# Top-k selection steps tied on VectorE behind mixer B's value evictions and key/query scalings

## The chip, the core and the metric

The kernel runs on one core of a Trainium2 chip. The metric is the device time of one execution in microseconds (us). Each kernel is run several times and the median is compared. Within a core, TensorE (PE) multiplies matrices into PSUM, VectorE (DVE) and ScalarE (ACT) work element by element, GpSimd (POOL) does the same more slowly and issues some transfers, and SyncE (SP) issues the others. Each engine works through its own list of instructions in order; semaphores tie the lists together.

## The reference

Two layers are computed on a sequence of 512 tokens of width 1024, in float32. A layer projects the normalised input with one wide matrix, feeds two attention mixers, merges them through sigmoid gates, and ends in a gated feed-forward part with a short convolution. What matters here is how the two mixers depend on the projection:

```python
# mixer A: sparse attention over the top 128 keys of each query
score = jnp.einsum('bths,bth->bts', rel, wi) * idx_scale
score = jnp.where(admissible[None], score, -jnp.inf)
_, sel = lax.top_k(score, topk)
...
# mixer B: latent attention, dense over the causal chunks
kv = (ckv @ b_w_ukv[l]).reshape(B, S, B_HEADS, B_NOPE + B_V)
kb = jnp.concatenate([kv[..., :B_NOPE], k_rope], axis=-1)
vb = kv[..., B_NOPE:]
qb = rms_norm(qb, b_q_norm[l])
kb = rms_norm(kb, b_k_norm[l])
y_b = latent_attention(qb, kb, vb)
```

The selection (`top_k`) needs only the indexer's scores, which are ready early in the layer, and its result is used only when mixer A starts. Mixer B lies between the two.

## The kernel before, in words

Every float32 product is split in a high and a low part, so that one product becomes three matmuls. PE therefore has a dense stream of matmuls with up to 512 columns. The low part of each operand is a subtraction on DVE (`split_into`, L312 to L318, `Weights.split`, L194), so that DVE stands behind nearly every operand that PE uses.

The program is written as several generators that are advanced in turn: a *filler* (`mix_dense`) that emits the projections piece by piece, the mixers (`scores_b`, `values`, `turn_b`), and the selection (`top_k`). A Tile scheduler then orders each engine's list by this emission order and by its own idea of when operands are ready. What an engine does next is thus set before the kernel runs, and the chip follows the lists.

In each layer this order holds around the change:

- The indexer's scores go into the tiles `sc`, for three query blocks with 512, 384 and 256 admissible keys. Block 0 needs no selection.
- `top_k` finds the 128 largest scores of each row, eight at a time, in 16 rounds. A round has six steps on DVE: three `V.max` (L1036, tile `m`), which find the eight largest, and three `V.match_replace` (L1043, tile `sc`), which mark them as taken. At the end three steps (L1047) turn the marks into the additive mask `sel`. These are 99 steps per layer.
- `side_0` hands out selection steps while the filler runs towards mark `b0`. It hands out `RATE_0` = 1 step for each piece of the filler. In this stretch lie four gate tiles `gb`, and then `attn_b(0)`, which makes mixer B's keys, values and queries for heads 0 to 3. Its four value tiles go through PSUM tag `L`, which has three banks. ACT copies the keys and the high part of the values, DVE takes the low part of the values (`vb`, L315), and the bank is free when both are done. The same banks hold the query tiles (L893) and later the attention scores.
- After that mixer B runs. `Feeder` advances the filler (the rest of `attn_b`, the gates, mixer A's first projections) and hands out `RATE_T` = 0.2 selection steps per call. Whatever is left is handed out before mixer A starts.
- `sel` is read first by POOL, in `bias_a` (L1115), for mixer A's first head.

Keys and queries are scaled on DVE (L880, tile `kn`, and L924, tile `qn`) and then transposed by PE (L1149), split (`tbh`, `tbl`), and multiplied into scores (L1164 to L1166). The rows' largest scores come from DVE (L1167, `mx`), the exponentials from ACT (L369, `P`), the division from DVE (L1063), and PE transposes the result (L1074).

Of the kernel before, what the change touches and what calls it, by code (L numbers as in the profile page):

```python
# [10 lines left out]
F32 = mybir.dt.float32  # L11
# [4 lines left out]
OP = mybir.AluOpType  # L16
# [23 lines left out]

RATE_B = [0.85, 0.55, 0.75, 0.55]
RATE_A = [0.95, 1.05, 0.65, 0.95]
RATE_T = 0.2
LAG_S = 22
LAG_T = 4
GAP_B = 12
# [17 lines left out]
VL = 0  # L64
TAIL = 1
TAIL_3 = 3
PK = 0
RATE_0 = 1
DL = ['gb', 'ga', 'uv', 'ug', 'kv', 'uq']
DN1 = []  # L70
DN2 = []
# [175 lines left out]
def trunk(ctx: ExitStack, tc: tile.TileContext, xT, wd, vecs, bias, rot_n, outT):  # L247
# [61 lines left out]
        split_into(h, o, src, scale, lag)  # L309
        return h, o  # L310

    def split_into(h, o, src, scale=None, lag=1):  # L312
        if scale is None:
            A.copy(h, src)
            later(lag, lambda: V.tensor_tensor(out=o, in0=src, in1=h.bitcast(F32), op=OP.subtract))  # L315
        else:
            A.activation(h, src, AF.Copy, scale=scale)
            later(lag, lambda: V.scalar_tensor_tensor(o, src, scale, h.bitcast(F32), op0=OP.mult, op1=OP.subtract))  # L318
# [253 lines left out]
    def mix_dense(l, nrm):  # L572
# [260 lines left out]
        def attn_b(g):  # L833
# [12 lines left out]
            while len(st.get("ckvl", ())) < 2:  # L846
                yield
            h, o = W.get("kv", g)
            for t in range(4):
                ts = slice(t * 128, (t + 1) * 128)  # L850
                p = bank(BB)
                xs = [(st["ckvh"][k][:, ts], st["ckvl"][k][:, ts]) for k in range(2)]
                seq = ([(x, h, k) for k in range(2) for x in xs[k]] + [(xs[k][0], o, k) for k in range(2)] if "k" in LO
                       else [q for k in range(2) for q in ((xs[k][0], h, k), (xs[k][1], h, k), (xs[k][0], o, k))])
                for n, (x, w, k) in enumerate(seq):
                    mm(p, lhsT=x, rhs=w[:, k * 512:(k + 1) * 512], start=n == 0, stop=n == 5, skip_group_check=True)
                    if n == 2:
                        yield
                if t == 3:
                    W.ahead()  # L860
                p = p.rearrange("p (h c) -> p h c", c=64)
                A.copy(k4[t][:, :, 0:64], p[:, 0:4])
                v = vb[t].rearrange("p (h c) -> p h c", c=128)
                split_into(v[:, :, 0:64], v[:, :, 64:128], p[:, 4:8])
                squares(p[:, 0:4], ssk[:, t], 64)
                yield

            def keys():
# [5 lines left out]
                def scale():  # L874
                    for t in range(4):
# [1 line left out]
                                        in0=st["kr"][:, t:t + 1, :].to_broadcast([128, 4, 32]),  # L877
                                        in1=r[:, t, :, None].to_broadcast([128, 4, 32]), op=OP.mult)
                        G.tensor_copy(k4[t][:, :, 96:100], late_k[:, t:t + 1, :].to_broadcast([128, 4, 4]))
                        (G if "K" in POOL else V).tensor_tensor(out=k4[t][:, :, 0:64], in0=k4[t][:, :, 0:64],  # L880
                                        in1=r[:, t, :, None].to_broadcast([128, 4, 64]), op=OP.mult)
                later(LAG_S, scale)
            later(3, keys)
# [32 lines left out]
            def queries():  # L916
# [4 lines left out]

                def scale():
                    for t in range(4):
                        (G if "Q" in POOL else V).tensor_tensor(out=q4[t][:, :, 0:96], in0=q4[t][:, :, 0:96],  # L924
                                        in1=r[:, t, :, None].to_broadcast([128, 4, 96]), op=OP.mult)
                later(LAG_S, scale)
            later(3, queries)
            st["b", g] = (qn, kn, vb)
# [100 lines left out]
    def top_k():  # L1029
# [3 lines left out]
        for _ in range(TOPK // 8):  # L1033
            for i in (3, 2, 1):
                with low():
                    ins = V.max(out=m8[i], in_=st["sc"][i][:, :128 * (i + 1)])  # L1036
                if PK and i == 3 and "v" in tables:
                    tc.add_manual_dep(ins.ins, tables["v"].ins.name, no_sync, reason="spread")
                yield
            for i in (3, 2, 1):  # L1040
                s = st["sc"][i][:, :128 * (i + 1)]
# [190 lines left out]
    for l in range(DEPTH):  # L1232
# [10 lines left out]

        fl.fill(GAP_I)
        weave([index_scores()], lambda: fl.fill(1))
        tk = top_k()

        def side_tk(n):
# [6 lines left out]
        due = [0.0]  # L1255

        def side_0():
            due[0] += RATE_0
            side_tk(int(due[0]))
            due[0] %= 1  # L1260

# [389 lines left out]
```

## Time and profile before

| what | value |
|---|---|
| time, median of 3 runs | 1537.66 us (1537.4 to 1538.77) |
| profiled execution | 1536.24 us, span 1534.5 us |
| PE busy | 1525.7 us (99% of the span) |
| PEld (weight load) busy | 1335.7 us (87%) |
| DVE busy | 1124.4 us (73%) |
| ACT busy, POOL busy | 946.3 us (62%), 396.3 us (26%) |
| granted TensorE clock | 1.00 |

Layer 0 lies at about 0 to 780 us of the span, layer 1 behind it. In layer 0 the selection runs from about 53 us to 177 us, mixer B's first value tile is multiplied at about 91 us, and mixer A's first head begins at about 224 us. In layer 1 the same stretch lies between about 810 us and 985 us.

A row of the timeline gives start and duration in us, then engine, line, operation, output and inputs, shape and count. Matmuls overlap, so that the distance from start to start, not the duration, is what one costs. In square brackets stands the idle time of the engine ahead of the row, and what ended it. A row of the windows gives, for a stretch, the busy time of PE, PEld, DVE, ACT and POOL, each with its count of instructions, then the granted clock, the DMA share and GB/s.

### The profile page before, as it was taken

What the parts mean: (1) busy time and instruction counts of PE and PEld (TensorE: products, weight loads), DVE (VectorE), ACT (ScalarE), POOL (GpSimd) and SP (SyncE); (2) the same over time, 40 slices, a digit from 0 to 9 for tenths busy, and PEclk for the clock granted to TensorE, in tenths of its full rate; (3) what the DMA queues carried; (4) which work ended last, traced back from release to release, by engine and by line L of the source; (5) the groups of instructions that cost most, each with busy time, mean ns of one, the idle gap of its engine ahead of it and who ended that gap; (6) DMA issues with size and microseconds to landing.
All of it is one profiled execution on the core that took longest, in us unless ns stands there. A gap on an engine that the chain in (4) does not pass through costs nothing.

```text
span 1534.5 us, 23946 instructions
## 1 busy us (share of the span) xinstructions
PE 1525.7 (99%) x8658; PEld 1335.7 (87%) x8658; DVE 1124.4 (73%) x2305; ACT 946.3 (62%) x1553; POOL 396.3 (26%) x578
## 2 busy tenths in 40 slices
PE   9999999999999999999999999999999999999999
PEld 8887999888888898889998889998888888988899
DVE  7899988666476693547979999886674857835586
ACT  7756668773577536664557576687635765456642
POOL 2343012400011442124602520223001115311364
PEclk9999999999999999999999999999999999999999
DMA  7464124733488438873454641356436783488732
GB/s 247 108 158 119 53 86 113 190 118 116 128 191 190 104 117 218 194 177 90 152 171 112 159 107 56 104 134 174 129 97 147 182 189 91 149 197 197 181 99 91
DMA packets 73575, 216.29 MB, mean 141 GB/s; under 512 B 8432, under 2 KB 11504, under 8 KB 73456
## 3 DMA queue, kind: packets, MB, share of 16 engines
q1 hardware_dynamic: 54592, 149.08, 30.7%
q0 software_dynamic: 18432, 65.28, 22.8%
q8 instruction: 68, 1.11, 0.3%
q14 instruction: 51, 0.42, 0.1%
q10 hardware_dynamic: 432, 0.40, 0.1%
HBM read 141.06 MB, written 4.19 MB: 95 GB/s over the span
## 4 chain that ended last, share of the span: by engine, by line
PE 86%; DVE 11%; ACT 2%; issue 1%; DMA 0%; SPq 0%; DVEq 0%; ACTq 0%
PE D L535 37%; PE T L535 15%; PE D L558 7%; PE L L1446 5%; PE T L1446 4%; PE D L1446 3%; DVE sc L1043 2%; PE Y L1081 2%; DVE m L1036 2%; PE Y L1446 2%; PE T L1074 2%; PE L L535 2%; PE L L336 1%; PE L L335 1%; PE L L728 1%
## 5 line engine op out<-in xcount | busy, mean ns | idle before, releaser
L182 ACT CAST wh<-wr 128x1024 fp32r<-128x1024 f32 (+2 forms) x205 | 211.3, 1034 | 163.7 <-PE D L535 73.8
L211 POOL DMA_DIRECT2D wl<-wr x128 | 110.7, 874 | 630.2 <-ACT wl L210 591.9
L535 PE MATMUL D<-hxh,wh 128*128 128x512 f32 (+1 forms) x440 | 174.0, 396 | 0.0
L535 PE MATMUL D<-hxl,wh 128*128 128x512 f32 (+1 forms) x440 | 172.8, 393 | 0.0
L210 ACT ACTIVATE wl<-wr 128x1024 fp32r<-128x1024 f32 (+2 forms) x128 | 132.2, 1035 | 48.1 <-PE D L535 25.9
L200 ACT CAST wh<-wr 128x896 fp32r<-128x896 f32 x88 | 82.6, 942 | 102.4 <-POOL wr L224 56.2
L1115 POOL TENSOR_TENSOR P<-M,sel 128x128 f32<-128x128 f32 (+1 forms) x64 | 53.4, 889 | 271.2 <-DMA M<-in_bias_dram 150.2
L535 PE MATMUL D<-hxh,wl 128*128 128x512 f32 (+1 forms) x440 | 117.8, 393 | 0.0
L224 POOL TENSOR_TENSOR wr<-wr 128x256 f32<-128x256 f32 x88 | 101.0, 1151 | 57.9 <-DVE wr L223 41.9
L558 PE MATMUL D<-wh,hxh 128*128 128x256 f32 x384 | 113.8, 297 | 0.0
L205 DVE TENSOR_TENSOR wl<-wr,wh 128x896 fp32r<-128x896 f32 x88 | 101.9, 1161 | 10.2 <-ACT wh L200 4.3
L558 PE MATMUL D<-wl,hxh 128*128 128x256 f32 x384 | 109.3, 285 | 0.0
L558 PE MATMUL D<-wh,hxl 128*128 128x256 f32 x384 | 108.4, 283 | 0.0
L535 PE MATMUL D<-hrl,wh 128*128 128x512 f32 x256 | 99.6, 389 | 0.0
L535 PE MATMUL D<-hrh,wh 128*128 128x512 f32 x256 | 99.6, 389 | 0.0
L535 PE MATMUL T<-hrh,wh 128*128 128x512 f32 x256 | 99.6, 389 | 0.0
L535 PE MATMUL T<-hrl,wh 128*128 128x512 f32 x256 | 99.6, 389 | 0.0
L194 DVE TENSOR_TENSOR wl<-wr,wh 128x1024 fp32r<-128x1024 f32 x77 | 94.9, 1238 | 6.3 <-ACT wh L182 5.6
L535 PEld LDWEIGHTS D<-hxh,wh 128*128 128x128 f32 x440 | 82.9, 188 | 13.4 <-DVE gb L702 0.2
L535 PEld LDWEIGHTS D<-hxl,wh 128*128 128x128 f32 x440 | 82.9, 188 | 12.7
L535 PEld LDWEIGHTS D<-hxh,wl 128*128 128x128 f32 x440 | 80.2, 188 | 14.0
L1390 DVE SCALAR_TENSOR_TENSOR c<-T,vec,c 128x511 f32<-128x511 f32 x32 | 23.9, 748 | 89.1 <-ACT c L1387 89.1
(458 smaller groups left out, 4571.4 us busy)
## 6 DMA issues: line engine op xcount, KB each, us to landing
wr<-in_wd_dram SPq DMA_DIRECT2D x197, 512.0 KB, 3.8
wl<-wr POOLq DMA_DIRECT2D x120, 512.0 KB, 5.4
wr<-in_wd_dram SPq DMA_DIRECT2D x88, 256.0 KB, 2.6
x<-in_xT_dram SPq DMA_DIRECT2D x16, 256.0 KB, 5.2
M<-in_bias_dram SPq DMA_DIRECT2D x16, 256.0 KB, 4.0
wr<-in_wd_dram SPq DMA_DIRECT2D x7, 384.0 KB, 3.2
kah<-kah SPq DMA_DIRECT2D x16, 128.0 KB, 4.3
kal<-kal SPq DMA_DIRECT2D x16, 128.0 KB, 3.8
```

What stands on the lines that cost most here:

```text
L182: ins = self.nc.scalar.copy(h[:, :n], t[:, :n])
L194: eng.tensor_tensor(out=o[:, c], in0=t[:, c], in1=h[:, c].bitcast(F32), op=OP.subtract)
L200: self.nc.scalar.copy(h[:, :896], t[:, 128:1024])
L205: self.later(lag, lambda: self.nc.vector.tensor_tensor(out=o[:, :896], in0=t[:, 128:1024], in1=h[:, :896].bitcast(F32), op=OP.subtract))
L210: self.nc.scalar.activation(o, t, AF.Copy, scale=-1.0)
L211: self.nc.gpsimd.dma_start(o.bitcast(F32), t, accum_op=OP.add)
L224: g(2)(out=b[:, 6:8], in0=b[:, 0:3:2], in1=b[:, 3:6:2], op=OP.add)
L535: mm(p[:, t0:], lhsT=w, rhs=x[:, t0:], start=n == 0, stop=n == len(seq) - 1, skip_group_check=True)
L558: mm(pp[b][:, t, :], lhsT=x, rhs=w, start=n == 0 and half == 0 and t == 0, stop=n == 11 and half == 1, skip_group_check=True)
L1036: ins = V.max(out=m8[i], in_=st["sc"][i][:, :128 * (i + 1)])
L1115: G.tensor_tensor(out=P[:, P0[i]:P0[i] + w], in0=M[:, 512 - w:512], in1=sel[:, SEL0[i]:SEL0[i] + w], op=OP.add)
L1446: mm(p, lhsT=w, rhs=x, start=b0, stop=b1, skip_group_check=True)
```

## The change

Four numbers and one tie are changed. The selection gets `RATE_0` = 1.55 steps per filler piece until mixer B's first value weight is taken (the new mark `values`), `RATE_1` = 0.5 from there to `b0`, and `RATE_T` = 0.25 during mixer B. With `PK` = 1 each `V.max` handed out is tied behind the latest instruction in `tables["hold"]`. That is the latest low part of a value tile (`last=True`), or the latest scaling of a key or query tile. The tie is an ordering on DVE's own list and adds no semaphore. A `match_replace` follows its own `V.max` through the data. `hold` is emptied when the selection starts, so that nothing is tied ahead of the first value tile. The choice of POOL for the scalings is dropped from the text; it was off before.

```diff
-RATE_T = 0.2
+RATE_T = 0.25
...
-PK = 0
-RATE_0 = 1
+PK = 1
+RATE_0 = 1.55
+RATE_1 = 0.5
...
-    def split_into(h, o, src, scale=None, lag=1):
+    def split_into(h, o, src, scale=None, lag=1, last=False):
         if scale is None:
             A.copy(h, src)
-            later(lag, lambda: V.tensor_tensor(out=o, in0=src, in1=h.bitcast(F32), op=OP.subtract))
+
+            def low():
+                ins = V.tensor_tensor(out=o, in0=src, in1=h.bitcast(F32), op=OP.subtract)
+                if last:
+                    tables["hold"] = ins
+            later(lag, low)
...
             h, o = W.get("kv", g)
+            done.add("values")
...
-                split_into(v[:, :, 0:64], v[:, :, 64:128], p[:, 4:8])
+                split_into(v[:, :, 0:64], v[:, :, 64:128], p[:, 4:8], last=True)
...
-                        (G if "K" in POOL else V).tensor_tensor(out=k4[t][:, :, 0:64], in0=k4[t][:, :, 0:64],
+                        tables["hold"] = V.tensor_tensor(out=k4[t][:, :, 0:64], in0=k4[t][:, :, 0:64],
                                         in1=r[:, t, :, None].to_broadcast([128, 4, 64]), op=OP.mult)
...
-                        (G if "Q" in POOL else V).tensor_tensor(out=q4[t][:, :, 0:96], in0=q4[t][:, :, 0:96],
-                                        in1=r[:, t, :, None].to_broadcast([128, 4, 96]), op=OP.mult)
+                        tables["hold"] = V.tensor_tensor(
+                            out=q4[t][:, :, 0:96], in0=q4[t][:, :, 0:96], in1=r[:, t, :, None].to_broadcast([128, 4, 96]), op=OP.mult)
...
                     ins = V.max(out=m8[i], in_=st["sc"][i][:, :128 * (i + 1)])
-                if PK and i == 3 and "v" in tables:
-                    tc.add_manual_dep(ins.ins, tables["v"].ins.name, no_sync, reason="spread")
+                if PK and "hold" in tables:
+                    tc.add_manual_dep(ins.ins, tables["hold"].ins.name, no_sync, reason="spread")
...
         weave([index_scores()], lambda: fl.fill(1))
+        tables.pop("hold", None)
         tk = top_k()
...
         def side_0():
-            due[0] += RATE_0
+            due[0] += RATE_1 if "values" in done else RATE_0
             side_tk(int(due[0]))
             due[0] %= 1
```

On DVE the change shows first at the values of heads 0 to 3, layer 0. This is DVE's list before, from the second value tile (`vb`) on; `ssk` are the sums of squares of the keys, `m` and `sc` the selection's steps.

```order
L315 TENSOR_TENSOR vb_1062<-L_1081,vb_1062 128x4x64
L844 TENSOR_REDUCE ssk_1065<-sqb_1092 128x4
L1036 MAX m_165_875<-sc_558 128x8
L315 TENSOR_TENSOR vb_1063<-L_1096,vb_1063 128x4x64
L844 TENSOR_REDUCE ssk_1065<-sqb_1107 128x4
L1036 MAX m_164_874<-sc_645 128x8
L1036 MAX m_163_873<-sc_752 128x8
L1043 MATCH_REPLACE sc_558<-m_165_875,sc_558 128x512
L1043 MATCH_REPLACE sc_645<-m_164_874,sc_645 128x384
L315 TENSOR_TENSOR vb_1064<-L_1111,vb_1064 128x4x64
```

And this is DVE's list from the same tile now (the line numbers are those of the changed kernel, 3 to 7 higher).

```order
L318 TENSOR_TENSOR vb_1080<-L_1098,vb_1080 128x4x64
L850 TENSOR_REDUCE ssk_1083<-sqb_1108 128x4
L318 TENSOR_TENSOR vb_1081<-L_1112,vb_1081 128x4x64
L850 TENSOR_REDUCE ssk_1083<-sqb_1122 128x4
L318 TENSOR_TENSOR vb_1082<-L_1126,vb_1082 128x4x64
L1043 MAX m_165_875<-sc_558 128x8
L850 TENSOR_REDUCE ssk_1083<-sqb_1143 128x4
L1043 MAX m_164_874<-sc_645 128x8
L877 TENSOR_TENSOR mk_1177<-ssk_1083,sskr_544 128x16
```

Five selection steps stood ahead of the fourth value tile, and now stand behind it.

The second place on DVE is the first value tile of heads 4 to 7, layer 0. The list before it (`y` and `t` are the Newton steps of the keys' inverse roots, `ssq` the sums of squares of the queries):

```order
L1043 MATCH_REPLACE sc_558<-m_165_875,sc_558 128x512
L356 SCALAR_TENSOR_TENSOR t_1168<-t_1168,mk_1164 128x16
L1043 MATCH_REPLACE sc_645<-m_164_874,sc_645 128x384
L357 SCALAR_TENSOR_TENSOR y_1167<-t_1168,y_1167 128x16
L1043 MATCH_REPLACE sc_752<-m_163_873,sc_752 128x256
L355 TENSOR_TENSOR t_1168<-y_1167 128x16
L1036 MAX m_165_875<-sc_558 128x8
L356 SCALAR_TENSOR_TENSOR t_1168<-t_1168,mk_1164 128x16
L1036 MAX m_164_874<-sc_645 128x8
L357 SCALAR_TENSOR_TENSOR y_1167<-t_1168,y_1167 128x16
L844 TENSOR_REDUCE ssq_1066<-sqb_1247 128x4
L315 TENSOR_TENSOR vb_1266<-L_1272,vb_1266 128x4x64
```

And now:

```order
L1050 MATCH_REPLACE sc_752<-m_163_873,sc_752 128x256
L362 SCALAR_TENSOR_TENSOR t_1181<-t_1181,mk_1177 128x16
L363 SCALAR_TENSOR_TENSOR y_1180<-t_1181,y_1180 128x16
L361 TENSOR_TENSOR t_1181<-y_1180 128x16
L362 SCALAR_TENSOR_TENSOR t_1181<-t_1181,mk_1177 128x16
L363 SCALAR_TENSOR_TENSOR y_1180<-t_1181,y_1180 128x16
L887 TENSOR_TENSOR kn_1071<-kn_1071,y_1180 128x4x64
L887 TENSOR_TENSOR kn_1072<-kn_1072,y_1180 128x4x64
L850 TENSOR_REDUCE ssq_1084<-sqb_1257 128x4
L887 TENSOR_TENSOR kn_1073<-kn_1073,y_1180 128x4x64
L318 TENSOR_TENSOR vb_1276<-L_1282,vb_1276 128x4x64
```

From the first value tile of heads 0 to 3 to this one, 16 selection steps stood in the list, and now 8; three key scalings (`kn`) have moved ahead of this tile.

The third place on DVE is the end of the selection, layer 0. Before, its last steps ended among the divisions and the low parts `ptl` of mixer B's fifth head (`P` scaled by `rs`):

```order
L1043 MATCH_REPLACE sc_645<-m_164_874,sc_645 128x384
L1056 RECIPROCAL rs_2155<-sm_2043 128x4
L1043 MATCH_REPLACE sc_752<-m_163_873,sc_752 128x256
L1063 TENSOR_SCALAR P_2042<-P_2042,rs_2155 128x128
L1063 TENSOR_SCALAR P_2042<-P_2042,rs_2155 128x256
L1063 TENSOR_SCALAR P_2042<-P_2042,rs_2155 128x384
L1047 TENSOR_SCALAR sel<-sc_558 128x512
```

Now they end around mixer A's first queries (`qae`, `qao`), among the low parts of mixer B's sixth head and behind:

```order
L1050 MATCH_REPLACE sc_558<-m_165_875,sc_558 128x512
L1050 MATCH_REPLACE sc_645<-m_164_874,sc_645 128x384
L1050 MATCH_REPLACE sc_752<-m_163_873,sc_752 128x256
L318 TENSOR_TENSOR ptl_2424<-T_2421,pth_2423 128x128
L1054 TENSOR_SCALAR sel<-sc_558 128x512
L334 TENSOR_TENSOR qae_2431<-T_2426,qae_2431 64x512
L335 TENSOR_TENSOR qao_2432<-T_2426,qao_2432 64x512
```

The end of the selection has moved back by one to two heads; its third step (256 keys) stands behind the seventh head's `rs`.

In layer 1 the lists move in the same way, except that ahead of its first value tile two selection steps more stand than before. SP's list and the counts of instructions on DVE, ACT, POOL and SP are unchanged; ACT, POOL and PE take the same work in a slightly different order.

## The prediction

> **What bounds the kernel now.** I read the page first, then the windows of 20 us, then PE's waits, then the timeline of PE and DVE at these waits.
>
> ```profile
> PE 1525.7 (99%) x8658; PEld 1335.7 (87%) x8658; DVE 1124.4 (73%) x2305; ACT 946.3 (62%) x1553; POOL 396.3 (26%) x578
> PE D L535 37%; PE T L535 15%; PE D L558 7%; PE L L1446 5%; PE T L1446 4%; PE D L1446 3%; DVE sc L1043 2%; PE Y L1081 2%; DVE m L1036 2%; PE Y L1446 2%; PE T L1074 2%; PE L L535 2%; PE L L336 1%; PE L L335 1%; PE L L728 1%
> ```
>
> PE is busy for 99% of the span, so over most of it nothing but fewer matmuls would help. But the chain of work that ended last leaves PE for 4% of its length and runs through the selection's own two lines, DVE `sc` L1043 and `m` L1036. There DVE decides, and the windows show where.
>
> ```profile
> 60.00:80.00 20.00, 20.00 (x100) 16.91 (x99) 20.00 (x49) 12.63 (x21) 5.34 (x5) 1.00 0.52 117
> 80.00:100.00 20.00, 19.51 (x88) 15.79 (x87) 20.00 (x61) 9.77 (x22) 5.01 (x13) 1.00 0.59 142
> 100.00:120.00 20.00, 19.08 (x95) 15.67 (x96) 20.00 (x76) 13.53 (x31) 16.32 (x48) 1.00 0.70 166
> 120.00:140.00 20.00, 19.38 (x104) 15.67 (x104) 19.70 (x57) 15.41 (x35) 8.95 (x22) 1.00 0.55 149
> 140.00:160.00 20.00, 19.84 (x116) 16.76 (x115) 19.87 (x45) 13.49 (x33) 0.00 (x0) 1.00 0.16 54
> 160.00:180.00 20.00, 20.00 (x161) 19.45 (x160) 18.76 (x48) 12.87 (x29) 0.00 (x0) 1.00 0.17 54
> 180.00:200.00 20.00, 19.75 (x158) 19.15 (x157) 18.43 (x44) 15.77 (x35) 0.00 (x0) 1.00 0.18 59
> 900.00:920.00 20.00, 20.00 (x116) 17.34 (x115) 19.66 (x45) 13.49 (x33) 0.00 (x0) 1.00 0.34 104
> 920.00:940.00 20.00, 20.00 (x159) 19.23 (x158) 18.09 (x45) 12.92 (x29) 0.00 (x0) 1.00 0.18 54
> 940.00:960.00 20.00, 19.75 (x161) 19.29 (x160) 18.43 (x43) 15.56 (x35) 0.00 (x0) 1.00 0.18 54
> ```
>
> From 60 to 160 us DVE is full, and this is the only long stretch of layer 0 where PE shows idle time: 0.49, 0.92, 0.62 and 0.16 us in the windows from 80 to 160 us, 2.2 us in all. The room for this change is therefore a few us out of 1536, and I price it wait by wait. PE's waits of the whole span name who ended them:
>
> ```profile
> PE L L856 <- DVE vb L315: 1.2, 3, 0.6
> PE L L1164 <- ACT P L369: 0.6, 1, 0.6
> PE L L893 <- DVE vb L315: 0.5, 1, 0.5
> PE T L1074 <- DVE P L1063: 0.4, 1, 0.4
> ```
>
> Four of them end with a value tile's low part on DVE, the very instructions behind which the selection is tied now.
>
> **The change part by part.** It adds and removes no instruction and no semaphore: DVE has 2211 rows in both lists. All it can do is change when DVE gets to the others.
>
> *First term, the value tiles.* PE waits here for a bank of tag `L`. Rows three and four are the wait for the fourth value tile, rows six and seven that for the fifth, the last two are layer 1's.
>
> ```profile
> 97.48 0.68 PE L893 MATMUL L<-wl,cqh 128*128 128x384 f32 x3
> 98.00 0.33 PE L893 MATMUL L<-wh,cqh 128*128 128x384 f32 x1
> 99.04 0.68 PE L893 MATMUL L<-wl,cqh 128*128 128x384 f32 x3
> 100.19 0.44 PE L893 MATMUL L<-wh,cqh 128*128 128x384 f32 x1 [0.46 <-DVE vb L315]
> 107.73 0.39 PE L856 MATMUL L<-wl,ckvh 128*128 128x512 f32 x1
> 107.96 0.39 PE L535 MATMUL D<-hxl,wh 128*128 128x512 f32 x1
> 108.94 0.50 PE L856 MATMUL L<-wh,ckvh 128*128 128x512 f32 x1 [0.59 <-DVE vb L315]
> 870.50 0.39 PE L535 MATMUL D<-hxh,wh 128*128 128x512 f32 x1
> 871.33 0.50 PE L856 MATMUL L<-wh,ckvh 128*128 128x512 f32 x1 [0.43 <-DVE vb L315]
> ```
>
> The same three 384-column matmuls take 0.52 us from start to start where nothing waits (97.48 to 98.00), and 1.15 us at 99.04, so 0.63 us is lost. A 512-column matmul takes 0.23 us (107.73 to 107.96), the one at 107.96 takes 0.98, so 0.75 is lost. At 870.50 it is 0.83, so 0.60 is lost. Sum 1.98 us. How much earlier does DVE come? A round of the selection costs, from start to start:
>
> ```profile
> 85.18 1.39 DVE m L1036 x3
> 87.15 1.59 DVE sc L1043 x3
> ```
>
> That is 2.98 us for six steps, 0.5 us a step. Five steps less ahead of the fourth tile are 2.5 us against 0.63 needed. Eight less ahead of the fifth are 4.0 us, of which the three key scalings that moved ahead take about 1.2 back (0.4 us each, as the like-sized `vb` quoted under the fourth term); 2.8 are left against 0.75. Both waits go. In layer 1 the difference at its fifth tile is only about 1 us, against 0.60. I take the whole 1.98 us; the other end is 0, should ACT's half of the eviction be what comes last then. The first wait of 0.2 us, ahead of all ties, stays.
>
> *Second term, the waits further on that a late DVE causes.*
>
> ```profile
> 131.83 0.39 PE L535 MATMUL D<-hxl,wh 128*128 128x512 f32 x1
> 132.78 0.50 PE L1164 MATMUL L<-tbh,tbh 100*128 100x512 f32 x1 [0.57 <-ACT P L369]
> 894.57 1.07 PE L535 MATMUL D<-hxh,wl 128*128 128x512 f32 x4
> 896.08 0.33 PE L1074 MATMUL T<-ident,P 128*128 128x128 f32 x1 [0.44 <-DVE P L1063]
> ```
>
> The first is 0.95 us instead of 0.23, so 0.72 is lost. It waits for an exponential on ACT, which itself waited for DVE's row maximum. The second is 1.51 us instead of four times 0.23, so 0.59. Sum 1.31 us. Counting DVE's lists row by row, the selection work ahead of the same instruction is smaller by 3 to 4 us at the query scalings of heads 0 to 3 and by 6.6 us (13 steps) at the first division of mixer B, in both layers. But part of this head start only becomes DVE idle time, because the scores cannot be earlier than PE makes them. I take 1.0 us, ends 0 and 1.31.
>
> *Third term, where the selection goes.* The 13 steps, 6.6 us, must be made up between the first division of mixer B and the new end of the selection. On DVE's list that end stands one to two heads later, right behind the second of these rows of before:
>
> ```profile
> 131.46 0.17 DVE L1056 RECIPROCAL rs<-sm 128x4 f32<-128x4 f32 x1
> ...
> 202.93 0.18 DVE L1056 RECIPROCAL rs<-sm 128x4 f32<-128x4 f32 x1
> ```
>
> So there are some 70 us for it. DVE's idle time on the way was 0.13 + 1.24 + 1.57 = 2.9 us between 140 and 200 us, and 0.34 + 1.91 + 1.57 = 3.8 us between 900 and 960. In the worst case all the head start has turned into idle time, and 3.7 and 2.8 us of DVE work find no cover: 6.5 us lost. In the best case DVE never idles and nothing is lost. Which end is nearer? Between 140 and 160 us DVE is already 99% full, with selection steps between mixer B's evictions, and PE still lost only 0.16 us there; a full DVE costs PE little as long as the evictions come in PE's order. The count of selection work ahead of any other instruction is never larger than before in layer 0, and meets it only at 203 us. So I take 1.0 us for both layers together, ends 0 and 6.5.
>
> *Fourth term, layer 1's first value tile.* Two more `V.max` stand ahead of it, because `RATE_0` = 1.55 hands the steps out faster up to there.
>
> ```profile
> 856.85 0.42 DVE L315 TENSOR_TENSOR vb<-L,vb 128x256 fp32r<-128x256 f32 x1
> 857.92 0.39 PE L856 MATMUL L<-wh,ckvh 128*128 128x512 f32 x1
> ```
>
> The tile's low part ended at 857.27 and PE took that bank again for the fourth tile at 857.92, so there were 0.65 us to spare. Two steps at 0.5 us take 1.0. I take 0.3 us lost, ends 0 and 0.5.
>
> *Nothing* is the price of the late `sel`. The last two of its three steps ended at 177.1 us, and POOL reads it first at 224.04 us, in an engine that had been idle for 93 us:
>
> ```profile
> 176.54 0.55 DVE L1047 TENSOR_SCALAR sel<-sc 128x384 bf16<-128x384 f32 x2
> 224.04 7.52 POOL L1115 TENSOR_TENSOR P<-M,sel 128x128 f32<-128x128 f32 x8 [93.69 <-DMA M<-in_bias_dram]
> ```
>
> With the end at about 203 us, 20 us of cover are left. If it were used up, each us beyond would delay mixer A by a us. SP's list is the same row by row. On POOL a few small key and query products change places with the transfers of weight low parts; that engine is busy for 9 of 20 us between 120 and 140 us and for none of the next 60, so I count nothing for it. The tie itself adds no wait: DVE reaches the `V.max` behind the held instruction in its list, and what stands behind a held instruction waits as it did before.
>
> The sum is -1.98 - 1.0 + 1.0 + 0.3 = -1.7 us on the profiled execution's 1536.24 us. That run was 1.4 us below the median of 1537.66 us, against which the result is measured; on the median the sum gives **1536.0 us**.
>
> By the Trainium skill (Trainium Kernel Development and Optimization, Best Practices) busy matmul time is a poor measure of distance to the roofline, and weight-load busy time a good one. Here PEld is 16.91 us in the last window before mixer B and 15.79, 15.67 and 15.67 in the next three; read as lost PE time this makes 3.6 us in layer 0 by an estimate from that page's rule, about 1.5 us more than the idle time in PE's own rows. Part of it is only that smaller matmuls come in, so I use it as an argument for the first rival alone.
>
> **The rivals.** *A. All waits go and nothing is given back.* The two sums are 3.3 us. At my three priced waits of layer 0 idle times of 0.46, 0.59 and 0.57 us cost 0.63, 0.75 and 0.72, some 0.16 us more each; by that the 2.2 us of idle time between 80 and 160 us cost about 2.8, which is 0.7 more than the 2.1 that I priced in layer 0. With a little for layer 1 I allow 1 us more. Time 1537.66 - 4.3 = 1533.4 us. For it speaks the 99% window that cost PE 0.16 us; against it, that DVE is the engine without slack and its work is unchanged.
>
> *B. Given back: no change.* DVE is full from 60 to 160 us, its work is the same, and PE cannot stay ahead of it. The 3 us won at the first and second term are lost again between 131 and 203 us. Time 1537.7 us. This is also the time if the tie does nothing on the chip, that is, if the waits at the value tiles are ended by ACT's copies instead.
>
> *C. Slower: DVE becomes the bound of mixer B's later heads.* The list now has a stretch of some 20 rows, around the fifth value tile, without selection steps. Where these rows wait for PE and ACT, DVE idles with nothing to fill in. If the whole 6.6 us of head start is lost that way, 6.5 us come late behind 140 us, and PE gains only the first term and half of the second: -2.6 + 6.5 + 0.3 = +4.2, 1541.9 us. It decides from about 3 us of new DVE idle time per layer between 94 and 142 us. Against it: 2.9 and 3.8 us of idle time are already there to take the steps.
>
> **How the numbers follow.** No change can be told from 0.2%, 3.1 us, so the bounds are 1534.6 and 1540.7 us. The forecast has 0.38 (nearly all of it inside the bounds), A 0.27, B 0.24, C 0.11. A lies below 1534.6; of the forecast 0.03 does as well. C is slower. That gives faster 0.30, same 0.59, slower 0.11. The forecast's own range is 1534.5 to 1537.5, from the ends of its terms without the far end of the third. To leave out no more than 2 in 10 the range reaches to A on one side and part of the way to C on the other: 1533.0 to 1539.0 us.
>
> **What would show it.** In the changed kernel PE's waits for `vb` should fall from 1.7 us to 0.2 or 0.3 (first term), and those for ACT `P` and DVE `P` should vanish (second). DVE's busy time should fall below 20 us in the windows from 100 to 140 us by up to 2 us in all, and rise in those from 160 to 200 us (third). A wait for `vb` of about half a us should appear at layer 1's fourth value tile (fourth). The last `sel` should end near 200 us. The prediction is wrong if DVE idles for more than 3 us per layer ahead of 142 us and PE shows new waits for `ptl`, `tbl` or `P` behind it (C), or if layer 0 is through mixer B more than 2.5 us earlier (A).

## The result and the profile after

The changed kernel takes 1546.64 us (median of 6 runs, 1545.65 to 1547.6), the kernel before, in runs beside it, 1537.75 us (6 runs, 1536.88 to 1538.77). The ratio is 1.0058, with a 95% interval of 1.0045 to 1.0071. The change makes the kernel slower by some 9 us, and the forecast of 1536.0 us with its range of 1533.0 to 1539.0 was wrong. The profiled run took 1547.6 us, with a span of 1545.9 us and a granted clock of 1.00.

The first line of the page of the changed kernel already says something that the forecast did not have. DVE executes the same 2305 instructions and is busy for 1132.9 us instead of 1124.4. Some instructions have become longer.

```profile
PE 1529.6 (99%) x8658; PEld 1335.2 (86%) x8658; DVE 1132.9 (73%) x2305; ACT 947.3 (61%) x1553; POOL 387.4 (25%) x578
```

The windows of the changed kernel show where DVE works (the busy times are those of PE, PEld, DVE, ACT and POOL).

```profile
80.00:100.00 20.00, 19.79 (x91) 16.31 (x90) 18.57 (x57) 9.98 (x21) 4.53 (x10) 1.00 0.55 138
100.00:120.00 20.00, 17.73 (x88) 14.41 (x87) 19.72 (x69) 12.10 (x28) 14.08 (x46) 1.00 0.71 169
120.00:140.00 20.00, 18.75 (x102) 15.07 (x101) 18.36 (x48) 16.53 (x35) 9.40 (x26) 1.00 0.52 131
...
160.00:180.00 20.00, 20.00 (x158) 19.13 (x156) 19.97 (x49) 12.86 (x30) 0.00 (x0) 1.00 0.16 54
180.00:200.00 20.00, 19.27 (x153) 18.32 (x153) 19.71 (x54) 14.31 (x32) 0.00 (x0) 1.00 0.17 54
200.00:220.00 20.00, 19.59 (x149) 18.31 (x148) 18.40 (x46) 15.12 (x33) 0.00 (x0) 1.00 0.26 81
```

From 80 to 140 us DVE now idles for 1.43 + 0.28 + 1.64 = 3.35 us, where it had idled for 0.30. From 160 to 200 us it has 0.32 us of idle time left, where it had 2.81. PE loses 3.7 us from 80 to 140 us, where it had lost 2.03, and 0.7 us from 180 to 200 us, where it had lost 0.25. PE's waits of the whole span name who ended them:

```profile
PE L L863 <- DVE vb L318: 3.4, 4, 2.0
PE L L1171 <- ACT P L375: 1.7, 2, 0.8
PE T L799 <- DVE ptl L318: 1.4, 3, 0.7
...
PE L L900 <- DVE vb L318: 0.8, 1, 0.8
PE Y L1088 <- DVE ptl L318: 0.7, 2, 0.4
```

The waits for `vb` have grown from 1.7 to 4.2 us, those for ACT `P` from 0.6 to 1.7, and the waits for `ptl`, which belong to mixer B's later heads and mixer A's beginning, are new. The timeline of PE shows the places: the fifth and the sixth value tile of layer 0, ACT's `P`, and the fourth and fifth value tile of layer 1.

```profile
107.44 0.40 PE L863 MATMUL L<-wl,ckvh 128*128 128x512 f32 x1
108.82 0.50 PE L863 MATMUL L<-wh,ckvh 128*128 128x512 f32 x1 [0.98 <-DVE vb L318]
...
110.09 0.39 PE L863 MATMUL L<-wl,ckvh 128*128 128x512 f32 x1
111.28 0.45 PE L900 MATMUL L<-wh,cqh 128*128 128x384 f32 x1 [0.81 <-DVE vb L318]
...
132.70 0.39 PE L541 MATMUL D<-hxl,wh 128*128 128x512 f32 x1
133.94 0.50 PE L1171 MATMUL L<-tbh,tbh 100*128 100x512 f32 x1 [0.85 <-ACT P L375]
...
864.61 0.39 PE L863 MATMUL L<-wl,ckvh 128*128 128x512 f32 x1
865.25 0.50 PE L863 MATMUL L<-wh,ckvh 128*128 128x512 f32 x1 [0.25 <-DVE vb L318]
...
877.57 0.39 PE L863 MATMUL L<-wl,ckvh 128*128 128x512 f32 x1
879.92 0.50 PE L863 MATMUL L<-wh,ckvh 128*128 128x512 f32 x1 [1.96 <-DVE vb L318]
```

By the distance from start to start, less 0.23 us for the matmul itself, 1.15, 0.96, 1.01, 0.41 and 2.12 us are lost here. The wait for the fourth value tile of layer 0 is gone.

To follow the loss through the program I matched each of ACT's instructions in two traces (same operation, tiles and shape, same number of them) and took the median shift of their starts, stretch by stretch. Between the two profiles the shift is 0.5 us ahead of 80 us, falls by 0.8 at the fourth value tile, is 2.0 us at 125 to 135 us and 5.4 us at 245 to 255. It grows by 0.7 us more up to 340 us and by 0.7 us around 750 us, at the end of layer 0, and in layer 1 from 6.9 to 11.4 us. So layer 0 lost 1.5 us around the values, keys and queries, and 3.5 us behind them. In layer 1 it is the other way round: 3.6 of its 4.5 us are lost up to 940 us, around the values, keys and queries and right behind them, and 0.9 later. The whole shift of 11.4 us is more than the 8.9 us between the medians, because it compares two single executions: the profiled one of the kernel before was 1.5 us below its median, that of the changed kernel 1.0 above. Shifts are therefore used for where time is lost, and the medians for how much.

### The profile page after: what moved, and what is told of

Same layout as the page of the kernel before. It is cut to its first block, busy times and chain, and to the rows that moved or that the text cites. A ratio compares the mean times of both kernels' runs of the same rounds, so it can differ in the third digit from the quotient of the medians.

```text
span 1545.9 us, 23941 instructions
## 1 busy us (share of the span) xinstructions
PE 1529.6 (99%) x8658; PEld 1335.2 (86%) x8658; DVE 1132.9 (73%) x2305; ACT 947.3 (61%) x1553; POOL 387.4 (25%) x578
## 4 chain that ended last, share of the span: by engine, by line
PE 71%; DVE 9%; ACT 2%; issue 1%; POOL 0%; DMA 0%; DVEq 0%; POOLq 0%; ACTq 0%
PE D L541 34%; PE T L541 15%; PE L L1454 4%; PE D L564 3%; PE T L1454 3%; PE D L1454 2%; PE L L541 2%; PE Y L1454 2%; PE Y L1088 2%; PE T L1081 1%; DVE sc L1050 1%; DVE m L1043 1%; DVE sc L1031 1%; PE L L342 1%; DVE wl L195 1%
## 5 line engine op out<-in xcount | busy, mean ns | idle before, releaser
L225 POOL TENSOR_TENSOR wr<-wr 128x256 f32<-128x256 f32 x88 | 93.5, 1066 | 63.3 <-DVE wr L224 46.8
```

Of the source, the lines that this page charges most:

```text
L225: g(2)(out=b[:, 6:8], in0=b[:, 0:3:2], in1=b[:, 3:6:2], op=OP.add)
```

## The experiments

Two theories stand against each other at first. **Deferral**: the tie and the slow pace push selection steps behind the first softmax tiles, where DVE is full, and DVE becomes the bound there (rival C of the prediction). **Key scalings**: with no selection steps to do, DVE runs the first group's key scalings ahead of the fifth value tile, and that tile comes late. A third is that the paces alone do it. The table gives the steps that stand, in DVE's list of layer 0, ahead of a value tile or of a row maximum of the softmax (four per head), the shift in layer 0 (early: from 80 to 95 us up to 125 to 135; late: from there up to 245 to 255 us), and the measured ratio to the kernel before.

| kernel | value tile 1, 5 | softmax tile 8, 16 | early, late (us) | ratio (95%) |
|---|---|---|---|---|
| before | 52, 68 | 79, 86 | 0, 0 | 1 |
| after | 52, 60 | 66, 76 | 1.5, 3.5 | 1.0058 (1.0045 to 1.0071) |
| `e1_pace_only` | 52, 68 | 79, 86 | 0.0, -0.1 | 1.0011 (1.0002 to 1.0021) |
| `e2_tie_only` | 36, 51 | 58, 67 | -1.7, 3.1 | 1.0033 (1.0021 to 1.0045) |
| `e3_tie_values` | 52, 60 | 73, 80 | 0.9, 0.4 | 1.0032 (1.0021 to 1.0043) |
| `e4_tie_scalings` | 52, 64 | 66, 77 | 0.8, 4.9 | 1.0070 (1.0055 to 1.0085) |
| `e5_keys_behind` | 52, 60 | 66, 76 | 0.1, 3.2 | 1.0046 (1.0031 to 1.0061) |
| `e6_tie_even` | 52, 68 | 76, 83 | 1.2, -0.5 | 1.0015 (1.0006 to 1.0025) |
| `e7_values_even` | 52, 68 | 80, 86 | 0.3, -0.5 | 1.0021 (1.0011 to 1.0030) |
| `e8_change_14` | 52, 60 | 66, 76 | 1.4, 0.2 | 1.0034 (1.0021 to 1.0047) |
| `e9_before_14` | 52, 68 | 79, 87 | 0.0, -0.2 | 1.0006 (0.9997 to 1.0016) |
| `e10_both_cures` | 52, 60 | 72, 78 | -0.5, 0.8 | 1.0012 (1.0003 to 1.0022) |
| `e11_values_48` | 48, 63 | 75, 82 | -0.9, 0.9 | 1.0009 (1.0000 to 1.0019) |
| `e12_pool_early` | 52, 60 | 66, 76 | 0.6, 3.4 | 1.0046 (1.0033 to 1.0060) |

### Paces alone, tie alone

```diff
-PK = 1
+PK = 0
```

> The three paces of the change (1.55, 0.5 and 0.25 for the two old ones of 1 and 0.2), no tie. In VectorE's order 52, 70, 79 and 86 selection steps stand ahead of the first value tile, the eighth, the eighth softmax tile and the sixteenth: the same as before. The theory of the tie (the tie causes the loss) expects 1537.7 within 1.5 us. The rival theory of the pace (0.5 steps a turn is too slow and pushes the steps to where VectorE is full) expects 1543 or more.

Measured 1539.09 us (1537.96 to 1539.63) against 1537.23. The paces alone cost 1.9 us, not 9. The tie is the cause of most of it, and the paces' part is looked at further down.

```diff
-RATE_T = 0.25
+RATE_T = 0.2
...
-RATE_0 = 1.55
-RATE_1 = 0.5
+RATE_0 = 1
+RATE_1 = 1
```

> The tie with the old paces (1, 1, 0.2). Only 36, 52, 58 and 67 steps stand ahead of the first value tile, the eighth, the eighth softmax tile and the sixteenth (after: 52, 62, 66, 76), and the fifth value tile comes ahead of all key scalings. The theory of deferral (what costs is the number of steps pushed behind the eighth softmax tile: 13 in the change cost some 3 us a layer between 190 and 252 us) expects 21 steps to cost more: 1548 to 1556, with VectorE idle between 60 and 100 us. The theory of the key scalings (what costs is that they stand ahead of the fifth value tile) expects 1541 to 1544. The theory of the pace expects 1538.

Measured 1542.53 us (1542.4 to 1543.93): the number of the key scalings, and too low for deferral as I had priced it. But the place of the loss is the one of deferral. These are windows of this kernel:

```profile
80.00:100.00 20.00, 20.00 (x94) 16.93 (x93) 13.06 (x40) 10.38 (x23) 4.98 (x13) 1.00 0.59 141
...
160.00:180.00 20.00, 20.00 (x164) 19.62 (x163) 19.94 (x50) 12.40 (x28) 0.00 (x0) 1.00 0.17 54
180.00:200.00 20.00, 19.05 (x148) 17.77 (x147) 19.86 (x54) 14.73 (x31) 0.00 (x0) 1.00 0.18 54
200.00:220.00 20.00, 19.70 (x148) 18.09 (x146) 19.57 (x50) 15.03 (x35) 0.00 (x0) 1.00 0.34 102
```

DVE idles for 6.94 us from 80 to 100 us, PE loses nothing there, and layer 0 gains 1.7 us up to 135 us, a gain of the kind that the forecast had promised. Then DVE has 0.63 us of idle time from 160 to 220 us, and 3.1 us are lost. What is not selected early is selected late.

### Which tie

```diff
-                        tables["hold"] = V.tensor_tensor(out=k4[t]...
+                        V.tensor_tensor(out=k4[t]...
...
-                        tables["hold"] = V.tensor_tensor(
+                        V.tensor_tensor(
```

> The change, but steps tied to value evictions alone, not to key and query scalings. The order is the change's up to the query scalings (key scalings ahead of the fifth value tile), then 73 steps ahead of the eighth softmax tile against 66. Deferral: half the late loss goes, 1542.5 to 1544.5. Key scalings: as the change within 1 us, 1545.5 to 1547.5.

Measured 1541.88 us (1540.86 to 1544.16), a little below deferral's range. The tie at key and query scalings is worth about half of the whole loss. With it goes the late loss (0.4 us instead of 3.5) and, in layer 0, the wait for ACT `P`; more than half of the early one stays.

```diff
-                split_into(v[:, :, 0:64], v[:, :, 64:128], p[:, 4:8], last=True)
+                split_into(v[:, :, 0:64], v[:, :, 64:128], p[:, 4:8])
```

> The change, but steps tied to key and query scalings alone, not to value evictions: VectorE has four steps to do ahead of the fourth value tile as before (no idle 1.4 us there), the key scalings ahead of the fifth value tile as in the change, 66 steps ahead of the eighth softmax tile as in the change. Deferral and key scalings both expect 1545.5 to 1548 (the 0.76 us gain at the fourth value tile is lost). If it is the idle time that the value tie opens on VectorE, 1543 or less.

Measured 1548.51 us (1546.59 to 1549.68), half a us above what both expected. The tie at the values is thus not what costs: without it the kernel is, if anything, slower.

### The key scalings behind the fifth value tile

```diff
+                        if g == 0:
+                            tc.add_manual_dep(tables["hold"].ins, tables["first"].ins.name, no_sync, reason="behind")
```

`first` is the low part of the second group's first value tile.

> The change, with the first group's key scalings put behind the fifth value tile's split on VectorE by an order-only dependency; the steps ahead of each value and softmax tile stay the change's within one (52, 61, 66, 76). The theory that the key scalings ahead of the fifth value tile cost the 2.2 us that ACT's rows show lost between 110 and 130 us in layer 0 expects 1542.5 to 1545. The theory that only the steps pushed behind the eighth softmax tile cost expects 1546 to 1548.

Measured 1543.88 us (1543.72 to 1545.38), in the range of the key scalings. The early loss of layer 0 falls from 1.5 to 0.1 us, and the late one stays at 3.2. The intervals of this run and of the change overlap, so the time alone does not prove the gain; the place does. The key scalings are the early loss of layer 0, and the smaller part of the whole.

### The same number of steps, tied

```diff
-RATE_T = 0.25
-RATE_1 = 0.5
+RATE_T = 0.2
+RATE_1 = 1
```

> The whole tie with paces of 1.55, 1 and 0.2: 52, 59, 68, 70 and 76 steps stand ahead of the first, fourth, fifth and eighth value tile and of the eighth softmax tile, against 52, 59, 68, 70 and 79 before, but spread behind the splits; all key scalings stand behind the fifth value tile. If deferral and key scalings are the whole loss, the early gain of the tie with the old paces (2.8 us in layer 0 up to 140 us) stays and its late loss of 4.3 us goes: 1533.5 to 1536.5. If holding steps behind key and query scalings costs by itself, as the 4.8 us between the change and the tie at values alone suggest: 1538 to 1542.

The same paces with the tie at values alone, as in `e3_tie_values`:

> As the run beside it, with paces of 1.55, 1 and 0.2, but steps tied to value evictions alone: the same order on VectorE up to the query scalings, 80 steps ahead of the eighth softmax tile. If deferral and key scalings are the whole loss: 1533.5 to 1536.5, within 1 us of the run beside it. If holding behind the scalings costs by itself: 3 us or more below the run beside it.

Measured 1539.62 us (1539.14 to 1541.67) and 1540.3 us (1539.36 to 1541.48). Both miss 1533.5 to 1536.5. The first lies in the range of the rival that the hold costs by itself (1538 to 1542), but the second should then be 3 us or more below it and is not, so this rival falls as well. With as many steps ahead as before the late loss is gone in both, but so is the early gain of `e2_tie_only`. That gain came from the 16 steps fewer ahead of the first value tile, not from where the steps stand between the tiles; `e11_values_48`, further down, bears this out. I had taken for a gain of the tie what was only work put off. The 2.4 and 3.1 us that remain arise in layer 1: there the shift grows by 2.7 and 3.7 us.

### Twelve steps left out

```diff
-        for _ in range(TOPK // 8):
+        for _ in range(TOPK // 8 - 2):
```

> The change with 14 of the 16 rounds of the selection in each layer: the last 12 steps of each layer (about 6.4 us of VectorE, all of them behind the sixteenth softmax tile in the change) are left out, so fewer keys are picked; everything ahead of them keeps its place (52, 54, 60, 62, 66, 76 steps as in the change). The theory of deferral (VectorE is full from 142 to 210 us, and late steps delay mixer B's last heads) expects the late loss of 3.5 us in layer 0 and some 2.5 us in layer 1 to go: 1539.5 to 1542. If the order of the steps costs by itself, whatever VectorE's load: 1545 to 1547.

> The kernel before with the same 12 steps a layer left out, as the measure for the run beside it. Its last 12 steps stand between the fourteenth and the twenty-fourth softmax tile, where VectorE still has idle time. The theory of deferral expects little: 1535 to 1537.5, so that change and before come to within 3 to 5.5 us of each other, against 9. If the steps cost the same wherever they stand, both kernels gain alike and the distance stays 8 to 10.

Measured 1542.71 us (1541.51 to 1543.62) and 1537.83 us (1537.12 to 1538.99). The two differ by 4.9 us, where change and before differ by 8.9. The distance is in deferral's range of 3 to 5.5, though each kernel lies above its own range, the first by 0.7 and the second by 0.3 us. These are windows of the change with 14 rounds:

```profile
160.00:180.00 20.00, 20.00 (x158) 19.13 (x156) 19.09 (x47) 12.86 (x31) 0.00 (x0) 1.00 0.17 54
180.00:200.00 20.00, 19.75 (x161) 19.28 (x161) 17.92 (x42) 15.57 (x33) 0.00 (x0) 1.00 0.17 54
```

From 160 to 180 us PE's numbers are those of the change. From 180 to 200 us DVE has 2.08 us of idle time again, PE is back at the 19.75 us it had before, and the late loss of layer 0 falls from 3.5 to 0.2 us. In the kernel before, leaving out the same 12 steps gains nothing (1.0006). This shows deferral: the last steps, made where DVE is full, cost 4 us of the 9. The table agrees over all kernels. With 66 steps or fewer ahead of the eighth softmax tile, and none left out, 3.1 to 4.9 us are lost late; with 72 or more, at most 0.9.

The part of the expectation on layer 1 failed. Some 2.5 us were to go there, but its shift still grows by 3.6 us, against 4.5 in the change, and 3.4 of them come up to 940 us. So deferral is the larger loss in layer 0, but in layer 1 most is lost at the values, keys and queries.

### Both cures, and a smaller early pace

The tie at values alone, together with the key scalings behind the fifth value tile, under the paces of the change:

> The change with its own paces, steps tied to value evictions alone, and the key scalings put behind the fifth value tile. If the two losses add, 4.7 us (tie at scalings, by the run tied at values alone) and 2.7 us (key scalings, by its run) go: 1538 to 1540.5. If they are one loss seen twice: 1541 to 1543.

Measured 1538.99 us (1537.31 to 1539.85), ratio 1.0012: the two losses add, and the growth of the shift in layer 1 falls to 1.2 us. The kernel is as fast as the paces without any tie (1.0011). So, within the intervals, the two losses are the whole price of the tie.

The tie at values alone with paces 1.4, 1 and 0.2:

> Steps tied to value evictions alone, paces 1.4, 1 and 0.2: 48, 54, 63, 65, 75 and 82 steps ahead of the first, fourth, fifth and eighth value tile and of the eighth and sixteenth softmax tile (before 52, 59, 68, 70, 79, 86; the run with 1.55: 52, 59, 68, 70, 80, 86, 1540.3). If waits at the value tiles follow the number of steps ahead of them (36, 42, 51, 52 steps gave a gain of 2.8 us in layer 0), and no late loss comes at 82 steps or more: 1535.5 to 1538. If the waits do not follow the number: 1539 to 1541.

Measured 1538.45 us (1538.01 to 1539.41), between the two ranges. The early gain is there (0.9 us) and is given back late (0.9 us), as deferral would have it. No kernel here is faster than the one before.

### Why the key scalings cost so much

The forecast had priced a key scaling at 0.4 us. The tile's own view gives minimum, median and maximum in ns, first before, then after:

```profile
L880 DVE TENSOR_TENSOR kn<-kn,y x16: 409/411/547, 108.9 to 885.5; 128x256 f32<-128x256 f32 x16
```

```profile
L887 DVE TENSOR_TENSOR kn<-kn,y x16: 421/618/1585, 106.3 to 894.0; 128x256 f32<-128x256 f32 x16
```

DVE's timeline of the changed kernel around the fourth, fifth and sixth value tile, and POOL's beside it:

```profile
99.14 0.43 DVE L318 TENSOR_TENSOR vb<-L,vb 128x256 fp32r<-128x256 f32 x1 [1.43 <-ACT sqb L849]
...
106.27 1.04 DVE L887 TENSOR_TENSOR kn<-kn,y 128x256 f32<-128x256 f32 x2
107.23 0.54 DVE L850 TENSOR_REDUCE ssq<-sqb 128x4 f32<-128x384 f32 x1
107.69 0.74 DVE L887 TENSOR_TENSOR kn<-kn,y 128x256 f32<-128x256 f32 x1
108.36 0.41 DVE L318 TENSOR_TENSOR vb<-L,vb 128x256 fp32r<-128x256 f32 x1
108.69 0.61 DVE L925 SCALAR_TENSOR_TENSOR mq<-ssq,ms 128x16 f32<-128x16 f32 x1
109.23 1.58 DVE L887 TENSOR_TENSOR kn<-kn,y 128x256 f32<-128x256 f32 x1
...
110.81 0.41 DVE L318 TENSOR_TENSOR vb<-L,vb 128x256 fp32r<-128x256 f32 x1
```

```profile
107.45 0.64 POOL L883 TENSOR_TENSOR kn<-kr,y 128x128 f32<-128x128 f32 x1
107.81 0.79 POOL L915 TENSOR_TENSOR qn<-qn,rotn 128x64 f32<-128x64 f32 x1
...
109.21 0.56 POOL L918 TENSOR_TENSOR qn<-qn,rot 128x64 f32<-128x64 f32 x1
109.49 0.98 POOL L883 TENSOR_TENSOR kn<-kr,y 128x128 f32<-128x128 f32 x2
```

Before, with selection steps between them, the same places on DVE, and POOL's row beside them, read:

```profile
108.47 0.41 DVE L315 TENSOR_TENSOR vb<-L,vb 128x256 fp32r<-128x256 f32 x1
108.80 0.16 DVE L918 SCALAR_TENSOR_TENSOR mq<-ssq,ms 128x16 f32<-128x16 f32 x1
108.89 0.41 DVE L880 TENSOR_TENSOR kn<-kn,y 128x256 f32<-128x256 f32 x1
```

```profile
108.80 0.70 POOL L909 TENSOR_TENSOR qn<-qn,rotn 128x64 f32<-128x64 f32 x1
```

In the changed kernel, beside POOL, instructions of DVE that read two tiles in SBUF become longer: a scaling takes 0.74 and 1.58 us instead of 0.41, the 16-column `mq` 0.61 instead of 0.16. `vb`, which reads one tile in PSUM and one in SBUF, and the sum `ssq`, which reads one tile, keep their 0.41 and 0.54 us. POOL's own instructions become longer, too. Before, POOL was also at work at this place, but there the scaling kept its 0.41 us and POOL's instruction was the one that became longer: 0.70 us, where the one ahead of it, of the same shape, took 0.32. By the Trainium skill (SBUF — State Buffer, Who interferes with whom) a DVE instruction with two SBUF inputs needs a read interface that it shares with GpSimd, and the order of issue decides which of the two is blocked; one with at most one SBUF input does not need it, unless it runs in a mode that uses both ports. The rows above agree with it. But a one-tile instruction was held as well (`y<-mq`, 1.33 us instead of 0.16; its row is shown under the second term below), and in which mode it ran no run here shows. A selection step has one input tile and keeps its duration in both kernels (a `match_replace` of 512 columns takes 0.67 to 0.69 us), and a key scaling has two. So the change put the second kind in the place of the first just while POOL turns the queries and scales its part of the keys. The last experiment takes a part of POOL's work away from there.

```diff
+                if g == 0:
+                    G.tensor_copy(k4[t][:, :, 64:96], st["kr"][...])
+                    G.tensor_copy(k4[t][:, :, 96:100], late_k[...])
...
-                        G.tensor_tensor(out=k4[t][:, :, 64:96], ...
+                        if g:
+                            G.tensor_tensor(out=k4[t][:, :, 64:96], ...
```

> The change, with POOL's part of the first group's keys (the scaled rotary columns and the late keys, eight instructions a layer) done as plain copies when the value tile comes, so that POOL does not do it while VectorE scales the keys; the rotary columns of that group stay unscaled. VectorE's order is the change's, instruction for instruction. In the change the fourth key scaling took 1.58 us and the third 0.74 us against 0.41 us before, while POOL worked on the same tiles. If the two engines hold each other up, the scalings come back towards 0.41 to 0.6 us, the waits of 0.98 and 0.81 us at the fifth and sixth value tile fall to 0.5 us or less each, and the time is 1543.5 to 1545.5. If the scalings' place alone costs: 1546 to 1548.

Measured 1544.71 us (1543.58 to 1547.25), in the range of the two engines holding each other up, though the intervals again overlap with the change's. DVE's timeline of this kernel:

```profile
107.21 0.90 DVE L891 TENSOR_TENSOR kn<-kn,y 128x256 f32<-128x256 f32 x1
...
108.78 0.46 DVE L891 TENSOR_TENSOR kn<-kn,y 128x256 f32<-128x256 f32 x1
```

The fourth scaling is back at 0.46 us, the sixth value tile's wait is gone, and the early loss falls from 1.5 to 0.6 us, with the same list on DVE. The third still takes 0.90 us, beside POOL's query rotation, which was left in place, and the fifth value tile still waits 1.06 us; there the expectation (0.5 us or less) was wrong.

### The paces' own 1.9 us

In `e1_pace_only` the shift is still 0.2 us where layer 1's front part begins (840 us), and there grows by 0.5 us at the first value tiles and by 1.2 us at 875 to 885 us. The second part is one instruction of DVE:

```profile
871.28 0.41 DVE L318 TENSOR_TENSOR vb<-L,vb 128x256 fp32r<-128x256 f32 x1
871.62 1.86 DVE L925 SCALAR_TENSOR_TENSOR mq<-ssq,ms 128x16 f32<-128x16 f32 x1
873.40 0.41 DVE L318 TENSOR_TENSOR vb<-L,vb 128x256 fp32r<-128x256 f32 x1
```

It has 16 columns, takes 0.16 us where nothing disturbs it, and here 1.86. It ends at 873.48 us, as POOL comes to the end (873.43) of an unbroken run of two-input instructions on the queries and keys:

```profile
870.78 0.50 POOL L883 TENSOR_TENSOR kn<-kr,y 128x128 f32<-128x128 f32 x1
...
872.61 0.82 POOL L883 TENSOR_TENSOR kn<-kr,y 128x128 f32<-128x128 f32 x2
```

In `e9_before_14`, which has the order of the kernel before at this place, the same `mq` took 1.87 us and the shift grew by 1.0 us, while in the kernel before it took 0.16. (Another `mq` of the kernel before, at 129.13 us, did take 1.26.) So a us or two in layer 1 depends on where POOL happens to be when DVE comes by. That this, and nothing else, is the price of the paces was not tried by a run of its own.

## Why the prediction was wrong, point by point

**What bounds the kernel** was read rightly: DVE is full from 60 to 160 us in the kernel before, and there and right behind it lies most of what was lost.

**First term (-1.98 us): wrong, +2.25.** The fourth value tile's 0.63 us went, as worked out. The 0.75 us at the fifth tile became 1.15 + 0.96, and layer 1's 0.60 became 2.12, together 4.23 us instead of 1.98. The step that failed is "eight less ahead of the fifth are 4.0 us, of which the three key scalings that moved ahead take about 1.2 back (0.4 us each)". DVE came to the fifth tile at 108.36 us instead of 108.47, 0.1 us earlier and not 2.8. Of the 4.0 us it had lost 1.43 waiting for ACT ahead of the fourth tile, 1.78 (not 1.2) to three scalings that POOL held up, and 0.48 because the whole program ran that much later; 0.2 us of it stay unexplained. In layer 1 two scalings in a row took 1.81 us at the same place. The fourth scaling, 1.58 us long, went ahead of the sixth tile, and the forecast had not counted it. The other end that I had named (ACT's half of the eviction comes last) is not what happened at the fifth tile, though DVE's 1.43 us of idle time was a wait for ACT.

**Second term (-1.0): wrong, +0.7.** The wait of 0.72 us for ACT `P` became 1.01 in layer 0. In layer 1 the wait of 0.59 us for DVE `P` went, but one for ACT `P` came in its place, with 0.82 us of idle time. The step that failed is "which itself waited for DVE's row maximum", and with it that fewer selection steps ahead would shorten the wait. ACT waited for the reciprocal `rs`, before (0.91 us ahead of 131.66) and after, and DVE came late to it: before behind a held `mq` and two selection steps, now behind a held `y<-mq` alone. These are rows of DVE, POOL and ACT after, and DVE's row before:

```profile
130.94 1.33 DVE L352 TENSOR_SCALAR y<-mq 128x16 int32<-128x16 int32 x1
...
132.61 0.17 DVE L1063 RECIPROCAL rs<-sm 128x4 f32<-128x4 f32 x1
```

```profile
131.78 0.45 POOL L918 TENSOR_TENSOR qn<-qn,rot 128x64 f32<-128x64 f32 x1
```

```profile
132.81 0.72 ACT L1068 ACTIVATE P<-P,rs 128x512 f32<-128x512 f32 x1 [1.01 <-DVE rs L1063]
133.44 0.35 ACT L375 ACTIVATE P<-L,mx 128x128 f32<-128x128 f32 x1
```

```profile
129.13 1.26 DVE L918 SCALAR_TENSOR_TENSOR mq<-ssq,ms 128x16 f32<-128x16 f32 x1
```

The 1.33 us end at 132.27 us, as POOL ends its query rotation (132.23). In each of the seven runs with the tie at scalings (`after` among them) `mq` or `y<-mq` is held for 1.32 to 1.39 us at this place, in both layers, and PE's waits for ACT `P` add up to between 1.0 and 1.7 us. In the four with the tie at values alone the longer of the two takes 0.16 to 1.10 us, and only `e3_tie_values` shows such a wait, of 0.7 us. That the hold makes the wait is read from these rows; no run changes it alone.

**Third term (+1.0, ends 0 and 6.5): the mechanism right, the size wrong.** The step that failed is "a full DVE costs PE little as long as the evictions come in PE's order". Leaving the last 12 steps out brings change and before 4 us closer. The late loss was 3.5 us in layer 0, next to the far end of 3.7 that the forecast had named and set aside, and 0.9 us in layer 1, where the far end was 2.8. The window from 140 to 160 us, on which I had chosen the low end, showed a full DVE that was still on time. From about 190 us on, after 50 us more of the same, its delay reached PE through `ptl`.

**Fourth term (+0.3): right.** Layer 1's fourth value tile waits 0.25 us, 0.41 by the starts of the matmuls, inside the ends of 0 and 0.5.

**The nothings.** The last `sel` of layer 0 started at 207.69 us, and POOL first reads it at 228.5: its cover held. (The 2.98 us of a selection round are the durations of its two rows added up, not a distance from start to start as the prediction says; the 0.5 us a step stand.) That the tie "adds no wait" missed that it takes away what DVE could do while it waits. That POOL counts for nothing was the largest gap: its busy time was looked at, not what it shares with DVE.

**The rivals.** C had the sign, the place and the test right. It was to decide from about 3 us of new DVE idle time per layer ahead of 142 us, and layer 0 shows 3.35 - 0.30 = 3.05 from 80 to 140 us. Its price of 4.2 us was half of what came, since it still counted the first term as a gain. It had 0.11. B's doubt (PE cannot stay ahead of DVE, whose work is unchanged) was the better guide to the first two terms: `e2_tie_only` and `e11_values_48` win early and give it back. A fell.

## What to carry to other kernels

On an engine that is full, a tie does not make work disappear: count the filler it removes as idle time where the engine waits, and charge the deferred work, less the idle time that it can still fill, at the first stretch where there is no slack left (3.7 us by that sum in layer 0, 3.5 measured). When filler goes, look at what moves up into its place, and at what the neighbouring engine does at that moment: an instruction with two SBUF inputs beside a busy POOL cannot be counted on to take its undisturbed duration. A window in which a full engine costs nothing says only that it is still on time.

## What the hardware showed that was not expected

POOL and DVE lengthen each other's two-input instructions: a 256-column scaling went from 0.41 to 1.58 us, POOL's scaling of its key columns from a median of 0.397 to 0.634 us, and a 16-column `mq` from 0.16 to 1.86 us, through several POOL instructions and not just one. Which of the two pays differs from place to place: in the kernel before, the longest of these POOL instructions took 2.18 us, beside four scalings of DVE (from 884.5 us on) that kept their 0.41. A `tensor_scalar` with one input tile was held as well (`y<-mq`, 1.33 us instead of 0.16), while reductions, selection steps and `vb` never were. The case of `mq` at 1.86 us shows up in a kernel whose list is that of the kernel before at this place, so that a fraction of a us in the phase between the two engines cost 1.0 us in that execution.
